# Seven products for eight: Strassen's algorithm in the first matrix of both MLPs, with two of four weight sums made by accumulating DMA transfers

## The chip, the cores and the metric

The kernel runs on one core of one Trainium2 chip. The metric is the device time of one execution in microseconds (us). PE is the matrix engine (TensorE) and PEld its weight load, ACT is ScalarE, DVE is VectorE, POOL is GpSimd, SP is the engine that issues most DMA transfers.

## The reference, cut to what matters

Two encoder layers over L = 16 + 512 tokens of width 1024. Each layer adds a mixer's output to the residual h, then an MLP's:

```python
u = rmsnorm(h, mlp_norm_g[layer])
h = h + jnp.square(jax.nn.relu(u @ w_ff1[layer])) @ w_ff2[layer]
return h[:, N_META:]
```

w_ff1 is 1024 x 4096 and w_ff2 is 4096 x 1024, in float32. The second layer's MLP works on the last 512 tokens only, since the others are dropped.

## The kernel before

Everything lies feature-major: a tile holds 128 features by all tokens. Every matrix product keeps nearly full float32 precision by splitting each operand into a rounded part and a remainder (xh and xl, wh and wl) and adding three products: wh·xh, wh·xl, wl·xh. A **unit** is one 128 x 1024 block of weights, 512 KB: SP loads `raw` (L207), ACT rounds it to `wh` (L208), DVE makes `wl` (L209), and `gemm` (L219) runs 8 k-steps x 3 products, in two halves of 264 tokens in the first layer (48 matmuls) or one piece of 512 tokens in the second (24).

The stages in order of time: the mixer of layer 0 (to 349 us), its output projection O0 (8 units), the MLP M0 (to 769 us), the mixer of layer 1, whose last part is the second half of its output projection (`c_out(4, KT)`, 8 half units), and the MLP M1 (974 us to the end).

An MLP runs in four quarters q of the hidden width. In each, 8 units of the first matrix W1 give 8 activation blocks (relu on ACT, times itself on DVE, then split into ah and al), and 8 units of the second matrix W2 use them; their results are added up in `facc` (L1133), and in the last quarter multiplied by `r2` (the squared norm factor, from `sum_squares` and a matmul with constants) and added to h. `make_x` (L1060, L1061) multiplies h by the norm's gain and splits it.

Tile pools give the memory: `wp` holds two buffers each of raw, wh and wl through the whole kernel. In PSUM, four tiles of two banks (`dn`) serve both MLPs. The text is written in a certain order, but a planner decides each engine's final order when the program is made: it takes the work that it expects to be ready, earlier text first, and an engine then runs its queue in order. A pool opened with `reuse_waits="tile"` over memory of a closed one waits tile by tile for what lay there.

Of the kernel before, what the change touches and what calls it, by code (L numbers as in the profile page):

```python
# [8 lines left out]
F32 = mybir.dt.float32  # L9
# [8 lines left out]
P = 128  # L18
# [116 lines left out]
def build(tc, ins, out, dbg=None):  # L135
# [14 lines left out]
    wp = ctx.enter_context(tc.tile_pool(name="wp", bufs=2, side="left"))  # L150
    xp = ctx.enter_context(tc.tile_pool(name="xp", bufs=1, side="left"))
    dp = ctx.enter_context(tc.tile_pool(name="dp", bufs=1, space=DRAM))

    psum = {}
# [46 lines left out]
    def load_unit(src):  # L201

        k, m = src.shape[1], src.shape[2]
        raw = wp.tile([P, k, m], F32, name="raw", tag="raw")
# [820 lines left out]
        tap(f"yA{h}", yA[h])  # L1025
    tap("yB", yB)
    ab_cm.__exit__(None, None, None)
    psum_pool("psm0", dn=4)
    if dbg is not None and "_ab" in dbg:
        for j in range(4):  # L1030
# [16 lines left out]
    hk = [h[:, k, :] for k in range(KT)]  # L1047
    yh, yl = [], []
    for k, s in enumerate(yA + [yB[:, j, :] for j in range(4)]):
        a, b = hl_tile(k, False), hl_tile(k, True)  # L1050
# [14 lines left out]
    def sum_squares(pool, t0=0):  # L1065

        sq = None
        for k in range(KT):
            s = pool.tile([P, L], F32, name="sqk", tag="sqk", bufs=2)
            S.activation(out=s[:, t0:], in_=hk[k][:, t0:], func=AF.Square)  # L1070
            if k:
                t = pool.tile([P, L], F32, name="sqa", tag="sqa", bufs=2)
# [5 lines left out]
    xs = []  # L1078
    for m in range(KT):
        hr = mp.tile([P, L], F32, name="hr", tag="hr", bufs=2)  # L1080
        nc.sync.dma_start(out=hr, in_=ins["h0"][:, m, :])
        ps = ps_dense()
        gemm(full(ps), load_unit(ins["w_o0"][m]), yh, yl)
        V.tensor_tensor(out=tokview(hk[m]), in0=ps[:, :, :HL], in1=tokview(hr), op=ALU.add)
        xs.append(make_x(m, PK_G + 8))
    yp_cm.__exit__(None, None, None)
    tap("h1", h)

    def mlp(layer, t0, xs, final):
        lp_cm = tc.tile_pool(name=f"mlp{layer}", bufs=1, side="right", reuse_waits="tile")  # L1090
        lp = lp_cm.__enter__()
        acc = lp.tile([P, KT, L], F32, name="facc")
        xh, xl = [x[0] for x in xs], [x[1] for x in xs]
# [10 lines left out]
        r2 = None  # L1104
        for q in range(4):
            ah, al = [], []
            for m in range(8):
                ps = ps_dense()
                gemm(dst(ps), load_unit(ins[f"w1_{layer}"][q * 8 + m]), xh, xl)
                rl = lp.tile([P, L], F32, name="rl", tag="rl", bufs=2)  # L1110
                S.activation(out=tview(rl), in_=pview(ps), func=AF.Relu)  # L1111
                V.tensor_tensor(out=tview(rl), in0=tview(rl), in1=pview(ps), op=ALU.mult)  # L1112
                a, b = hl_tile(m, False), hl_tile(m, True)
                S.copy(out=a[:, t0:], in_=rl[:, t0:])  # L1114
                V.tensor_tensor(out=b[:, t0:], in0=rl[:, t0:], in1=a[:, t0:], op=ALU.subtract)  # L1115
                ah.append(a)
                al.append(b)
            if q == 1:
                sq = sum_squares(lp, t0)
# [5 lines left out]
                V.reciprocal(out=r2[:, t0:], in_=r2[:, t0:])  # L1125
            for m in range(8):
                ps = ps_dense()
                gemm(dst(ps), load_unit(ins[f"w2_{layer}"][q * 8 + m]), ah, al)
                ak = acc[:, m, :]
                if q == 0:  # L1130
                    S.copy(out=tview(ak), in_=pview(ps))
                else:
                    V.tensor_tensor(out=tview(ak), in0=tview(ak), in1=pview(ps), op=ALU.add)  # L1133
                if q == 3:
                    V.tensor_tensor(out=ak[:, t0:], in0=ak[:, t0:], in1=r2[:, t0:], op=ALU.mult)
                    V.tensor_tensor(out=hk[m][:, t0:], in0=hk[m][:, t0:], in1=ak[:, t0:], op=ALU.add)
                    final(m)
        lp_cm.__exit__(None, None, None)

    mark("M0")  # L1140
    xs2 = []
    mlp(0, 0, xs, lambda m: xs2.append(make_x(m, PK_G + 16)))
    tap("h2", h)
    xh, xl = [x[0] for x in xs2], [x[1] for x in xs2]


    mark("L1")
    psum_pool("psc", dn=2, pw=2, po=1, cq=1)
    cp_cm = tc.tile_pool(name="cp", bufs=1, side="right", reuse_waits="tile")
    cp = cp_cm.__enter__()  # L1150
    rope = cp.tile([P, 2, L], F32, name="rope")
# [1 line left out]
    cst_ = {}  # L1153

    def stats():
        sq = sum_squares(cp)
# [141 lines left out]
        yl.append(b)  # L1298
        yield

    xs = []

    def c_out(k0, k1):

        for m in range(KT):
            mark("O1")
            ps = ps1("cq") if k0 == 0 else ps1(("cq", "po")[m % 2])
            gemm([(ps, slice(NM, L))], load_unit(ins["w_o1"][m][:, k0:k1, :]), yh[k0:k1], yl[k0:k1])
            V.tensor_tensor(out=hk[m][:, NM:], in0=ps, in1=hk[m][:, NM:], op=ALU.add)
            if k1 == KT:  # L1310
                xs.append(make_x(m, PK_G + 24, NM))
            yield


# [5 lines left out]
    next(streams["k0"])  # L1320
    stats()
    trace(streams, ORDER_C)
    weave((c_out(4, KT), 1))
    cp_cm.__exit__(None, None, None)
    tap("h3", h)

    psum_pool("psm1", dn=4)
    mark("M1")
    mlp(1, NM, xs, lambda m: nc.sync.dma_start(out=out[m], in_=hk[m][:, NM:]))
    psum_pool(None)  # L1330
    ctx.close()

# [74 lines left out]
```

## Time and profile before

| | us |
|---|---|
| median of 3 runs (1334.22, 1339.44, 1339.55) | 1339.44 |
| the profiled execution | 1335.85 |
| its span, first to last instruction | 1334.1 |
| PE busy in the span | 1299.1 (97%) |
| DVE busy | 754.9 (57%) |
| ACT busy | 558.6 (42%) |

Matmuls are pipelined, so the busy time of one is longer than the distance to the next. That distance, here called the pitch, is what a stream of matmuls costs for each.

### The profile page before, as it was taken

To read this page: it belongs to the slowest core of one execution; us is meant where nothing else is said; L and a number is where in the kernel's file an instruction comes from. 1 tells how busy PE (TensorE), PEld (TensorE's weight loads), DVE (VectorE), ACT (ScalarE), POOL (GpSimd) and SP (SyncE) were. 2 spreads that over 40 slices of the span, in tenths; PEclk is the share of its full clock that TensorE was granted. 3 is DMA by queue.
4 is the path that set the end of the run, shared out by engine and by line. 5 is a ranking of instruction groups with operands and counts; after the bars stand their busy time and mean duration, and the time that the engine had idled before them with its cause. 6 is when DMAs were issued, how large, how long until landed. Compare 5 with 4: busy or idle time off the path is not lost.

```text
span 1334.1 us, 21206 instructions
## 1 busy us (share of the span) xinstructions
PE 1299.1 (97%) x8595; PEld 1180.8 (89%) x8595; DVE 754.9 (57%) x1575; ACT 558.6 (42%) x1084; POOL 88.1 (7%) x202
## 2 busy tenths in 40 slices
PE   7998999899999999999999999999999999999998
PEld 6997999789899999999999987988788888888886
DVE  5686868986554324434335668698663244343444
ACT  4634565556533323223123357576443232231331
POOL 1051506030000000000000000000000000000000
PEclk9998999999899999999999999999999999999999
DMA  4321212100143323332332221101243333333333
GB/s 170 113 64 32 65 33 65 48 2 3 49 126 95 96 83 93 95 91 85 95 96 87 88 85 43 56 16 33 71 117 94 98 95 92 95 95 102 95 97 98
DMA packets 32081, 105.20 MB, mean 79 GB/s; under 512 B 3688, under 2 KB 3816, under 8 KB 31856
## 3 DMA queue, kind: packets, MB, share of 16 engines
q1 hardware_dynamic: 31984, 103.86, 25.9%
q8 instruction: 67, 1.10, 0.4%
q14 instruction: 30, 0.25, 0.1%
HBM read 101.73 MB, written 2.11 MB: 78 GB/s over the span
## 4 chain that ended last, share of the span: by engine, by line
PE 88%; DVE 5%; ACT 3%; POOL 2%; issue 1%; DMA 1%; SPq 0%; ACTq 0%; DVEq 0%
PE dn L219 64%; PE cq L219 5%; PE po L1292 2%; PE dn L1265 2%; PE pw L980 1%; PE pw L1286 1%; POOL u L634 1%; DVE cy L429 1%; POOL ut L633 1%; PE po L219 1%; PE rw L735 1%; PE rw L668 1%; PE rw L682 1%; PE pw L464 1%; PE rw L723 1%
## 5 line engine op out<-in xcount | busy, mean ns | idle before, releaser
L208 ACT CAST wh<-raw 128x1024 fp32r<-128x1024 f32 (+1 forms) x186 | 188.3, 1012 | 479.9 <-PE dn L219 416.7
L209 DVE TENSOR_TENSOR wl<-raw,wh 128x1024 fp32r<-128x1024 f32 (+1 forms) x186 | 219.9, 1182 | 254.0 <-ACT wh L208 249.5
L219 PE MATMUL dn<-xh,wh 128*128 128x264 f32 (+1 forms) x1184 | 297.4, 313 | 1.1 <-ACT wh L208 0.9
L219 PE MATMUL dn<-xh,wl 128*128 128x264 f32 (+1 forms) x1184 | 294.4, 312 | 0.0
L219 PE MATMUL dn<-xl,wh 128*128 128x264 f32 (+1 forms) x1184 | 294.3, 310 | 0.0
L219 PE MATMUL dn<-ah,wh 128*128 128x264 f32 (+1 forms) x896 | 232.3, 318 | 0.0
L219 PE MATMUL dn<-ah,wl 128*128 128x264 f32 (+1 forms) x896 | 230.6, 316 | 0.0
L219 PE MATMUL dn<-al,wh 128*128 128x264 f32 (+1 forms) x896 | 229.4, 314 | 0.0
L219 PEld LDWEIGHTS dn<-xl,wh 128*128 128x128 f32 x1184 | 195.7, 191 | 12.1
L219 PEld LDWEIGHTS dn<-xh,wh 128*128 128x128 f32 x1184 | 195.3, 191 | 12.4 <-issue 1.1
L219 PEld LDWEIGHTS dn<-xh,wl 128*128 128x128 f32 x1184 | 194.0, 190 | 11.1 <-issue 0.2
L219 PEld LDWEIGHTS dn<-al,wh 128*128 128x128 f32 x896 | 148.3, 189 | 11.9 <-issue 0.2
L219 PEld LDWEIGHTS dn<-ah,wh 128*128 128x128 f32 x896 | 148.0, 190 | 10.8 <-ACT ah L1051 0.3
L219 PEld LDWEIGHTS dn<-ah,wl 128*128 128x128 f32 x896 | 147.0, 188 | 11.0
L1133 DVE TENSOR_TENSOR facc<-facc,dn 128x528 f32<-128x528 f32 (+1 forms) x48 | 33.3, 693 | 129.8 <-PE dn L219 129.8
L1114 ACT CAST ah<-rl 128x528 fp32r<-128x528 f32 (+1 forms) x64 | 40.1, 627 | 89.3 <-DVE rl L1112 89.3
L1115 DVE TENSOR_TENSOR al<-rl,ah 128x528 fp32r<-128x528 f32 (+1 forms) x64 | 44.8, 701 | 43.2 <-ACT ah L1114 43.0
L1112 DVE TENSOR_TENSOR rl<-rl,dn 128x528 f32<-128x528 f32 (+1 forms) x64 | 44.1, 689 | 0.0
L429 DVE SCALAR_TENSOR_TENSOR cy<-cin,pk,cy 128x526 f32<-128x526 f32 (+1 forms) x48 | 38.2, 797 | 1.3 <-ACT cy L426 1.0
L1111 ACT ACTIVATE rl<-dn 128x528 f32<-128x528 f32 (+1 forms) x64 | 38.2, 597 | 0.0
L633 POOL TENSOR_TENSOR ut<-abc,u 128x150 f32<-128x150 f32 (+14 forms) x60 | 29.8, 497 | 93.8 <-DVE abc L625 89.5
L1224 POOL MEMSET cvt<- 128x128 f32 x2 | 0.4, 204 | 526.2 <-PE pw L457 526.2
(447 smaller groups left out, 1726.9 us busy)
## 6 DMA issues: line engine op xcount, KB each, us to landing
raw<-in_w SPq DMA_DIRECT2D x128, 512.0 KB, 3.6
raw<-in_w_in SPq DMA_DIRECT2D x22, 512.0 KB, 3.7
raw<-in_w_c SPq DMA_DIRECT2D x12, 512.0 KB, 3.6
raw<-in_w_o SPq DMA_DIRECT2D x8, 512.0 KB, 3.7
raw<-in_w_o SPq DMA_DIRECT2D x16, 256.0 KB, 2.7
gcb<-gdram SPq DMA_DIRECT2D x8, 264.0 KB, 4.5
hr<-in_h SPq DMA_DIRECT2D x8, 264.0 KB, 2.7
out<-h SPq DMA_DIRECT2D x8, 256.0 KB, 2.0
```

The lines of the kernel that those rows point to most:

```text
L208: S.copy(out=wh, in_=raw)
L209: V.tensor_tensor(out=wl, in0=raw, in1=wh, op=ALU.subtract)
L219: T.matmul(o, a[:, k, :], b[k][:, sl], start=first and k == 0 and i == 0, stop=last and k == n - 1 and i == 2)
L429: V.scalar_tensor_tensor(out=y[:, a:a + n], in0=x[:, b:b + n], scalar=w(j), in1=y[:, a:a + n], op0=ALU.mult, op1=ALU.add)
L633: G.tensor_tensor(out=ut[:, :, :, :n], in0=arow, in1=ucol, op=ALU.mult)
L1111: S.activation(out=tview(rl), in_=pview(ps), func=AF.Relu)
L1112: V.tensor_tensor(out=tview(rl), in0=tview(rl), in1=pview(ps), op=ALU.mult)
L1114: S.copy(out=a[:, t0:], in_=rl[:, t0:])
L1115: V.tensor_tensor(out=b[:, t0:], in0=rl[:, t0:], in1=a[:, t0:], op=ALU.subtract)
L1133: V.tensor_tensor(out=tview(ak), in0=tview(ak), in1=pview(ps), op=ALU.add)
L1265: T.matmul(ps[:, s, :HL], a[:, sl], b[:, s * HL:(s + 1) * HL], start=i == 0, stop=i == 2)
L1292: T.matmul(po, a[:, kc, :], b, start=kc == 0 and i == 0, stop=kc == NC and i == 2)
```

## The change

For each pair of W1 units, seen as 2 x 2 blocks (two column blocks of weights, two halves of the 1024 inputs) against 2 x 2 blocks of the input (two halves of the inputs, two halves n of the tokens: n = 264 in the first layer, 256 in the second), Strassen's algorithm in Winograd's form takes 7 products of half size for 8. Each product still has three matmuls for each of 4 k-steps.

The sums of inputs (T1 to T4) are made once, by `Fast.add`, in O0 and in `c_out`. The sums of weights are made for each pair: two by accumulating DMA transfers that GpSimd issues onto blocks which SP loaded, two on DVE. The results come together from PSUM: ACT copies partial sums out (e0 to e3), and PE goes on accumulating on the same bank. h is parked in DRAM during the MLP and read back by GpSimd's queue, and the W2 sums use h's own memory in the place of `facc`. Weight pools are now opened and closed stage by stage; the MLP's has 5 buffers for wh and wl.

```diff
+    def weight_pool(name, bufs=2):
+        if "cm" in wpool:
+            wpool.pop("cm").__exit__(None, None, None)
+        if name is not None:
+            wpool["cm"] = tc.tile_pool(name=name, bufs=bufs, side="left", reuse_waits="tile")
+            wpool["p"] = wpool["cm"].__enter__()
+        return wpool["p"]
...
+        def add(self, k):
...
+            if k < 4:
+                x = self.temp.tile([P, L], F32, name=f"xf{k}")
+                S.activation(out=x[:, t0:], in_=hk[k][:, t0:], func=AF.Copy, scale=g)
+                self.split("B11", i, a[:, t0:m], b[:, t0:m], x[:, t0:m])
+                self.first[i] = x
+                V.tensor_tensor(out=x[:, t0:m], in0=x[:, t0:m], in1=x[:, m:], op=ALU.subtract)
+                self.split("T1", i, a[:, m:], b[:, m:], x[:, t0:m])
+                return
+            x, hs = self.first.pop(i), hk[k]
+            S.activation(out=a[:, t0:], in_=hs[:, t0:], func=AF.Copy, scale=g)
+            V.scalar_tensor_tensor(out=b[:, t0:], in0=hs[:, t0:], scalar=g, in1=a[:, t0:], op0=ALU.mult, op1=ALU.subtract)
...
+            V.scalar_tensor_tensor(out=t2, in0=hs[:, m:], scalar=g, in1=x[:, t0:m], op0=ALU.mult, op1=ALU.add)
+            self.split("T2", i, *part("T2"), t2, -1.0)
+            V.scalar_tensor_tensor(out=t3, in0=hs[:, m:], scalar=g, in1=x[:, m:], op0=ALU.mult, op1=ALU.subtract)
+            self.split("T3", i, *part("T3"), t3)
+            V.scalar_tensor_tensor(out=t4, in0=hs[:, t0:m], scalar=g, in1=t2, op0=ALU.mult, op1=ALU.subtract)
+            self.split("T4", i, *part("T4"), t4, -1.0)
...
+            def load(name, i):
+                raw = wp.tile([P, 3, 4, P], F32, name="raw", tag="raw", bufs=2)
+                w = ins[f"{name}_{layer}"]
+                nc.sync.dma_start(out=flat(raw[:, 0:2]), in_=w[i])
+                if name == "w2":
+                    return raw, None
+                s = wp.tile([P, 4, 4, P], F32, name="sums", tag="sums", bufs=2)
+                nc.sync.dma_start(out=s[:, 1], in_=w[i][:, :4])
+                nc.sync.dma_start(out=s[:, 2], in_=w[i + 1][:, 4:])
+                nc.sync.dma_start(out=raw[:, 2], in_=w[i + 1][:, 4:])
+                for k in (1, 2):
+                    G.dma_start(out=s[:, k], in_=w[i + 1][:, :4], accum_op=ALU.add)
+                return raw, s
...
+                yield split(flat(raw[:, 0:2]))
+                if w == "w2":
+                    continue
+                V.tensor_tensor(out=s[:, 3], in0=s[:, 2], in1=raw[:, 0], op=ALU.add)
+                yield split(flat(s[:, 2:4]))
+                V.tensor_tensor(out=s[:, 0], in0=s[:, 3], in1=raw[:, 1], op=ALU.add)
+                yield split(flat(s[:, 0:2]))
+                yield split(raw[:, 2])
...
+        def product(o, g, half, name, start):
+            wh, wl = groups[g]
+            for k in range(4):
+                xh, xl = fast.ops[name][k]
+                for i, (a, b) in enumerate(((wh, xh), (wh, xl), (wl, xh))):
+                    T.matmul(o, a[:, half * 4 + k, :], b, start=start and k == 0 and i == 0, stop=k == 3 and i == 2, skip_group_check=not start)
+        def activated(m, c):
+            S.activation(out=c[:, t0:], in_=c[:, t0:], func=AF.Square)
+            a, b = hl_tile(m, False), hl_tile(m, True)
+            S.copy(out=a[:, t0:], in_=c[:, t0:])
+            V.tensor_tensor(out=b[:, t0:], in0=c[:, t0:], in1=a[:, t0:], op=ALU.subtract)
+            return a, b
+        def pair(base, m, before):
...
+            prepare()
+            product(pa, base, 0, "B11", True)
+            S.copy(out=e[0], in_=pa)
+            product(pb, base, 1, "B21", True)
+            used.add(base)
+            V.tensor_tensor(out=c0[:, lo], in0=e[0], in1=pb, op=ALU.add)
+            before()
+            prepare()
+            product(pa, base + 1, 1, "T2", False)
+            S.copy(out=e[1], in_=pa)
+            product(pd, base + 1, 0, "T1", True)
+            used.add(base + 1)
+            S.copy(out=e[2], in_=pd)
+            prepare()
+            product(pa, base + 2, 1, "T3", False)
+            S.copy(out=e[3], in_=pa)
+            V.tensor_tensor(out=c1[:, hi], in0=e[3], in1=e[2], op=ALU.add)
+            product(pd, base + 2, 0, "B22", False)
+            used.add(base + 2)
+            S.activation(out=c1[:, hi], in_=c1[:, hi], func=AF.Relu, scale=-1.0)
+            V.tensor_tensor(out=c0[:, hi], in0=e[1], in1=pd, op=ALU.add)
+            S.activation(out=c0[:, t0:], in_=c0[:, t0:], func=AF.Relu)
+            acts[m] = activated(m, c0)
+            def end():
+                prepare()
+                product(pa, base + 3, 0, "T4", False)
+                used.add(base + 3)
+                S.activation(out=c1[:, lo], in_=pa, func=AF.Relu, scale=-1.0)
+                acts[m + 1] = activated(m + 1, c1)
+            return end
...
+                if q == 3:
+                    o = lp.tile([P, L], F32, name="last", tag="c0", bufs=2)
+                    V.tensor_tensor(out=tview(o), in0=tview(r2), in1=pview(ps), op=ALU.mult)
+                    V.tensor_tensor(out=ak[:, t0:], in0=ak[:, t0:], in1=o[:, t0:], op=ALU.add)
                     final(m)
```

`prepare` takes the next groups of split weights while fewer than 5 are open; `pair` is called with the former pair's `end` as `before`, so that the product T4 of a pair stands among the next pair's.

## Rows read from the trace of the kernel before

**Rows 1.** Busy time of each engine in M0 and in M1, clock, DMA.

```profile
core 0: us, PE busy (x) PEld busy (x) DVE busy (x) ACT busy (x) POOL busy (x), PEclk, DMA share, GB/s
398.00:769.00 371.00, 371.00 (x3076) 370.87 (x3075) 156.75 (x177) 113.94 (x145) 0.00 (x0) 1.00 0.31 91
974.20:1329.20 355.00, 354.76 (x1538) 288.30 (x1537) 149.16 (x172) 106.82 (x137) 0.00 (x0) 1.00 0.32 97
```

**Rows 2.** Chain of work that ended last, in order of time: start, duration, count.

```profile
537.80 231.26 PE dn L219 x1918
...
974.19 133.12 PE dn L219 x576
...
1108.17 220.80 PE dn L219 x960
```

**Rows 3.** The same chain in the mixer of layer 1: transposes of 128 columns.

```profile
939.42 0.87 PE pw L1286 x8
940.29 2.96 PE cq L219 x12
```

**Rows 4.** ACT, groups by shape: count, busy us, mean ns, idle time before.

```profile
L208 ACT CAST wh<-raw 128x1024 fp32r<-128x1024 f32 x170 | 178.3, 1049 | 461.3 <-PE dn L219 416.7 <-issue 38.5 <-PE cq L219 3.2
...
L1114 ACT CAST ah<-rl 128x528 fp32r<-128x528 f32 x32 | 20.3, 634 | 44.7 <-DVE rl L1112 44.7
...
L1111 ACT ACTIVATE rl<-dn 128x528 f32<-128x528 f32 x32 | 19.3, 604 | 0.0
...
L208 ACT CAST wh<-raw 128x512 fp32r<-128x512 f32 x16 | 9.9, 621 | 18.6 <-PE cq L219 15.6 <-ACT sqk L1070 3.0
L1070 ACT ACTIVATE sqk<-h 128x528 f32<-128x528 f32 x16 | 9.8, 633 | 0.8 <-DVE sqa L1073 0.8
...
L319 ACT COPY gt<-rw 32x264 f32<-32x264 f32 x2 | 0.7, 368 | 6.3 <-PE rw L318 6.3
```

**Rows 5.** DVE, groups by shape.

```profile
L209 DVE TENSOR_TENSOR wl<-raw,wh 128x1024 fp32r<-128x1024 f32 x170 | 208.9, 1229 | 254.0 <-ACT wh L208 249.5 <-PE dn L1122 2.5
...
L1115 DVE TENSOR_TENSOR al<-rl,ah 128x528 fp32r<-128x528 f32 x32 | 22.7, 708 | 21.8 <-ACT ah L1114 21.7
...
L1061 DVE SCALAR_TENSOR_TENSOR xl<-h,pk,xh 128x528 fp32r<-128x528 f32 x16 | 12.2, 765 | 6.4 <-ACT xh L1060 6.4
L209 DVE TENSOR_TENSOR wl<-raw,wh 128x512 fp32r<-128x512 f32 x16 | 10.9, 683 | 0.0
...
L592 DVE TENSOR_TENSOR dt<-pw,dt 128x256 f32<-128x256 f32 x16 | 6.1, 413 | 0.0
...
L1084 DVE TENSOR_TENSOR h<-dn,hr 128x528 f32<-128x528 f32 x8 | 5.7, 708 | 20.6 <-PE dn L219 20.6
```

**Rows 6.** ACT's timeline, four casts in a row.

```profile
348.08 2.22 ACT L1051 CAST ah<-yA 128x528 fp32r<-128x528 f32 x4
```

**Rows 7.** DVE's timeline, four subtractions in a row.

```profile
349.26 2.56 DVE L1052 TENSOR_TENSOR al<-yA,ah 128x528 fp32r<-128x528 f32 x4
```

**Rows 8.** ACT's timeline where O0 passes into M0.

```profile
398.83 0.73 ACT L1060 ACTIVATE xh<-h,pk 128x528 fp32r<-128x528 f32 x1
399.47 0.63 ACT L1070 ACTIVATE sqk<-h 128x528 f32<-128x528 f32 x1
403.66 1.05 ACT L208 CAST wh<-raw 128x1024 fp32r<-128x1024 f32 x1 [3.57 <-issue]
404.62 0.60 ACT L1111 ACTIVATE rl<-dn 128x528 f32<-128x528 f32 x1
```

**Rows 9.** DMA issues by line: KB each, median us from issue to landing.

```profile
raw<-in_w SPq DMA_DIRECT2D x128, 512.0 KB, 3.6
...
raw<-in_w_o SPq DMA_DIRECT2D x16, 256.0 KB, 2.7
gcb<-gdram SPq DMA_DIRECT2D x8, 264.0 KB, 4.5
```

**Rows 10.** SP's timeline in O0: a W1 unit's load.

```profile
382.85 0.33 SPq L207 DMA_DIRECT2D raw<-in_w  x1
```

**Rows 11.** Busy time and clock where the first mixer ends.

```profile
340.00:352.00 12.00, 9.68 (x58) 7.98 (x57) 6.47 (x24) 8.79 (x28) 0.00 (x0) 0.81 0.00 1
```

More of the change, by code (lines that the diff above doesn't have):

```diff
@@ L1047, in build @@
     hk = [h[:, k, :] for k in range(KT)]
+    hdram = [dp.tile([P, KT, L], F32, name=f"hdram{i}") for i in range(2)]
     yh, yl = [], []
@@ L1063, in make_x, with __init__, split @@
         return a, b
-    def sum_squares(pool, t0=0):
+    class Fast:
+        def __init__(self, pool, temp, gcol, t0):
+            self.pool, self.temp, self.gcol, self.t0, self.n = pool, temp, gcol, t0, (L - t0) // 2
+            self.first, self.ops = {}, {n: [None] * 4 for n in ("B11", "B21", "B22", "T1", "T2", "T3", "T4")}
+        def split(self, name, i, a, b, src, sign=1.0):
+            S.activation(out=a, in_=src, func=AF.Copy, scale=sign)
+            if sign == 1.0:
+                V.tensor_tensor(out=b, in0=src, in1=a, op=ALU.subtract)
+            else:
+                V.scalar_tensor_tensor(out=b, in0=src, scalar=sign, in1=a, op0=ALU.mult, op1=ALU.subtract)
+            self.ops[name][i] = (a, b)
+        def add(self, k):
+            t0, n, g = self.t0, self.n, pkc(self.gcol + k)
+            m, i = t0 + n, k % 4
+            a = xp.tile([P, L], F32R, name=f"xh{k}", tag=f"xh{k}")
+            b = xp.tile([P, L], F32R, name=f"xl{k}", tag=f"xl{k}")
+            fresh = lambda name: self.temp.tile([P, HL], F32, name=name, tag=name, bufs=2)[:, :n]
+            part = lambda name: [self.pool.tile([P, HL], F32R, name=f"{name}{c}{i}")[:, :n] for c in "hl"]
+            if k < 4:
[9 more added lines that the diff above has]
+            V.scalar_tensor_tensor(out=b[:, t0:], in0=hs[:, t0:], scalar=g, in1=a[:, t0:], op0=ALU.mult, op1=ALU.subtract)
+            self.ops["B21"][i] = (a[:, t0:m], b[:, t0:m])
+            self.ops["B22"][i] = (a[:, m:], b[:, m:])
+            t2, t3, t4 = fresh("t2"), fresh("t3"), fresh("t4")
+            V.scalar_tensor_tensor(out=t2, in0=hs[:, m:], scalar=g, in1=x[:, t0:m], op0=ALU.mult, op1=ALU.add)
[4 more added lines that the diff above has]
+            self.split("T4", i, *part("T4"), t4, -1.0)
@@ L1076, in sum_squares, with park @@
         return sq
-    xs = []
+    def park(layer, k, t0=0):
+        G.dma_start(out=hdram[layer][:, k, t0:], in_=hk[k][:, t0:])
+    fq_cm = tc.tile_pool(name="fq0", bufs=1, side="left", reuse_waits="tile")
+    fq = fq_cm.__enter__()
+    ft_cm = tc.tile_pool(name="ft0", bufs=1, side="left", reuse_waits="tile")
+    fast = Fast(fq, ft_cm.__enter__(), PK_G + 8, 0)
+    weight_pool("wo0")
     for m in range(KT):
@@ L1102, in tview, with reload @@
             return tokview(ap) if t0 == 0 else ap[:, t0:]
-        r2 = None
-        for q in range(4):
[L1106 to L1117, printed above, removed]
+        def reload(m):
+            o = mp.tile([P, L], F32, name="hr", tag="hr", bufs=2)[:, t0:]
+            G.dma_start(out=o, in_=hdram[layer][:, m, t0:])
+            return o
@@ new lines, in weight_groups, with split @@
+        def weight_groups():
+            def split(src):
+                k = src.shape[1]
+                wh = wp.tile([P, KT, P], F32R, name="wh", tag="wh", bufs=RING)
+                wl = wp.tile([P, KT, P], F32R, name="wl", tag="wl", bufs=RING)
+                S.copy(out=wh[:, :k], in_=src)
+                V.tensor_tensor(out=wl[:, :k], in0=src, in1=wh[:, :k], op=ALU.subtract)
+                return wh, wl
+            def load(name, i):
[11 more added lines that the diff above has]
+                return raw, s
+            flat = lambda t: t.rearrange("p a k m -> p (a k) m")
+            todo = []
+            for q in range(4):
+                todo += [("w1", q * 8 + m) for m in range(0, 8, 2)] + [("w2", q * 8 + m) for m in range(8)]
+            loaded = [load(*todo[0])]
+            for i, (w, m) in enumerate(todo):
+                if i + 1 < len(todo):
+                    loaded.append(load(*todo[i + 1]))
+                raw, s = loaded.pop(0)
+                yield split(flat(raw[:, 0:2]))
[6 more added lines that the diff above has]
+                yield split(raw[:, 2])
@@ new lines, in mlp, with prepare @@
+        source = weight_groups()
+        groups, used = [], set()
+        def prepare():
+            while len(groups) < RING or len(groups) - RING in used:
+                g = next(source, None)
+                if g is None:
+                    return
+                groups.append(g)
+        def product(o, g, half, name, start):
[4 more added lines that the diff above has]
+                    T.matmul(o, a[:, half * 4 + k, :], b, start=start and k == 0 and i == 0, stop=k == 3 and i == 2, skip_group_check=not start)
@@ L1118, in mlp @@
+        r2, base = None, 0
+        for q in range(4):
+            acts = {}
+            end = lambda: None
+            for m in range(0, 8, 2):
+                end = pair(base, m, end)
+                base += 4
+            end()
             if q == 1:
-                sq = sum_squares(lp, t0)
+                sq = sum_squares(lp, reload, ("c0", "c1"))
                 ps = ps_dense()
@@ L1155, in stats @@
     def stats():
-        sq = sum_squares(cp)
+        sq = sum_squares(cp, lambda k: hk[k])
         ps = ps_dense()
@@ L1310, in c_out @@
             if k1 == KT:
-                xs.append(make_x(m, PK_G + 24, NM))
+                park(1, m, NM)
+                fast.add(m)
             yield
```

66 lines of the change are left out of this document (49 added, 17 removed).

## The prediction

> **What bounds the kernel now.** I first read the busy time by stage. In both MLPs PE is busy for practically the whole stretch (371.00 of 371.00 us, 354.76 of 355.00), at the full granted clock, while ACT and DVE are busy for less than half of it [rows 1]. The chain of waits says the same: through both MLPs it runs along L219 almost without a break [rows 2]. So an MLP lasts as long as its matmuls take, and a matmul that is left out is worth one pitch, as long as the other engines keep up and nothing new stops PE.
>
> The pitch comes from the chain: 231.26 us for 1918 matmuls of 264 columns is 120.6 ns; (133.12 + 220.80) us for 576 + 960 of 512 columns is 230.4 ns [rows 2]. A line through both has 0.443 ns a column, and gives 117.0 ns at 256 columns, a width that no MLP row has.
>
> Last I read the order on ACT's queue, since the change hangs on it. A cast of weights (403.66) runs ahead of the relu (404.62) that stands before it in the text, and a square of `sum_squares`, written after the second quarter, runs at 399.47 in O0 [rows 8]. So the planner doesn't keep the written order; it fills an engine with what is ready.
>
> **What is removed.** A pair of W1 units had 96 matmuls in M0 and has 84 (7 products x 4 k-steps x 3). There are 16 pairs: 16 x 12 x 0.1206 = 23.1 us. In M1 a pair had 48 matmuls of 512 columns, 11.06 us, and gets 84 of 256: 84 x 0.1170 = 9.83 us, so 16 x 1.23 = 19.7 us. Bounds for M1: if the cost went by columns alone (0.1152), 22.1 us; if 256 columns cost as much as 264, 14.9 us. Would the weight load set the pitch, since M1 now loads weights 84 times and not 48? Eight transposes, each with fresh weights, go by in 0.87 us, 109 ns apart [rows 3], below 117. Together 42.8 us.
>
> The Trainium skill (TensorE: Matmul & The Clock Gate, section Back-to-back issue gap) puts an isolated gap at N/2.4 + 2.5 ns, which would be 112.5 ns at 264 columns and 109.2 at 256. By it the saving would be 40.6 us as an estimate. The measured pitch [rows 2] is 7% longer at 512 and 264 alike, and I take the rows.
>
> The last unit's tail gets shorter: one DVE pass in place of a sum (0.708, [rows 5]) at the end of either MLP, 1.4 us.
>
> **What ACT and DVE must do in a pair's time.** By durations [rows 4, 5], for a pair in M0. ACT: three casts of 1024 columns (3.147), one of 512 (0.621), six operations on 264 columns (e0 to e3 and two relus, 2.208 by the row of 264), a relu (0.604), two squares and two casts of 528 (2.534): 9.11 us. DVE: three remainders of 1024 (3.687), one of 512 (0.683), two weight sums (1.366), three sums of 264 (1.239 by the row of 256), two remainders of 528 (1.416): 8.39 us. PE needs 84 x 0.1206 = 10.13. Operations in a row overlap: four casts took 2.22 us, 0.53 apart for 0.63 each [rows 6], and four subtractions 2.56, 0.62 apart for 0.70 [rows 7]. With 0.10 off each of 15 operations and 0.08 off each of 11, ACT needs 7.6 us and DVE 7.5. Both fit, at three quarters of PE's time, where they are under half now. If their work is hidden it costs nothing; but PE now waits for them inside a pair: T3 goes onto the bank that e1 is copied from, and only T1 (12 x 0.1206 = 1.45 us) lies between. A copy takes 0.37 us, an unlucky cast of 1.05 ahead of it makes 1.42, and with the handing over PE stops for a few tenths, unless it has the next pair's B11 to do. Bounds: nothing, and 1.0 us a pair. I take 0.2, since the order is by readiness: 32 x 0.2 = 6.4 us.
>
> **The transfers in the steady state.** A pair now loads 1.25 MB by SP and 0.5 MB by GpSimd, where it loaded 1 MB. The DMA engines' share of 0.31 [rows 1] becomes 0.31 x 1.75 x 11.58 / 10.13 = 0.62. An accumulating transfer of 256 KB is in no row: between a plain one, 2.7 us, and the slowest of that size, 4.5 [rows 9]. SP's loads can start when the buffers of two pairs ago are free; with groups split five ahead, that is two pairs and three products, 2 x 10.13 + 4.3 = 24.6 us, before T2 reads the first sum. Casting and summing take 3.0 of it. Loads and both accumulations one after another take at most 3.6 + 3 x 2.7 + 2 x 4.5 = 20.7. So they are hidden. Behind an accumulation on GpSimd's queue stand only the parked h and the next accumulation. The loads of h for the squares and for the third quarter's sum go past with slack of several units.
>
> **Where PE stops: the two entries.** Now W1's first weights are loaded during O0 (382.85, [rows 10]) from a pool that stays. After the change the MLP's pool is opened over `Fast.add`'s temporaries and the closed projection pool, and waits for them tile by tile. In the order of allocation, the memory for sums lies over the temporaries t3 and t4 and over O0's raw weights. After the last matmul of O0 (398.0) these take h 0.708, xh 0.73, xl 0.765, then T2 to T4 with six more operations of 0.41 and one of 0.37 on the way, some 4.6 us [rows 5, 8]. Then a load (2.7), the accumulations (2.7 to 4.5), and sum, cast and remainder (0.683 + 1.049 + 1.229 = 2.96): T2 can start 13.0 to 14.8 us after O0. PE has the two products B11 and B21 of the first pair and of the next to do, 5.8 us; it stops for 7 to 9. Bounds: 0 if the memory doesn't collide, 12 if the next pair isn't taken ahead. I take 8.
>
> At M1 the sums' memory lies over the projection's last weights, free when PE is done with them: 2.7 + 2.7 to 4.5 + 2.96 = 8.4 to 10.2 us, less 4 x 12 x 0.117 = 5.6 of products. Besides, `add` costs DVE in the last four half units of `c_out` about 4.6 us each (0.683 for the weights, 0.683, 0.765, six of 0.41), against 12 x 0.2304 = 2.77 on PE: DVE comes 4.5 (back to back) to 7.4 us late into M1. I take 6, from 3 to 12. O0 itself opens a new pool too: load, cast and remainder, 3.6 + 1.05 + 1.23 = 5.9 us at most; its memory is that of tiles used some us before the first mixer's end, so I take 0.
>
> Where PE had been idle, 9.68 busy of 12.00 us, the granted clock was 0.81 [rows 11], a mixture of the levels 2.4 and 1.2 GHz. The stops at the entries should show this too. I add 2 us, from 0 to 4. The Trainium skill says the same of idleness (TensorE: Matmul & The Clock Gate, Part 1: The HAM clock gate); it adds no term.
>
> **The sum**, against the profiled execution: 1335.85 - 42.8 - 1.4 + 6.4 + 8 + 6 + 2 = 1314.0. The median lies 3.6 us above that execution (1339.44), so 1317.6, rounded to 1318 us.
>
> **Rivals.**
>
> *ACT and DVE set the pair's time (slower or the same).* In the written order each engine would wait for the other, from one T4 to the next: relu 0.368, square 0.633, cast 0.634, cast 1.049, remainder 1.229, sum 0.683, cast 1.049, remainder 1.229, sum 0.683, cast 1.049, remainder 1.229, two sums 0.826, relu 0.604, square 0.633, cast 0.634, cast 0.621, copy 0.368: 13.52 us, against 11.58 and 11.06 now. With 12 of 16 pairs so (the last of a quarter prepares W2's weights, the first has no former T4), 12 x (1.94 + 2.46) = 52.8 lost, the other pairs' gain of 4 x (1.45 + 1.23) = 10.7 kept: 1335.85 + 52.8 - 10.7 - 1.4 + 16 + 3.6 = 1396. Rows 8 speak against it in full. In part it can be: the planner goes by expected durations, and engines keep its order when the real ones differ. It decides from (42.8 + 1.4 - 16) / 32 = 0.88 us lost a pair; at 1.3 us the time is 1353. Chance 0.20.
>
> *The entries are hidden (faster still).* If the first loads find free memory, no more than 3 us is left of the entries and clock: 1335.85 - 42.8 - 1.4 + 6.4 + 3 + 3.6 = 1305, with 1299 where no pair loses anything. Against it: a pool of three times the former size can't lie clear of what was just closed. Chance 0.12.
>
> *The sums come late.* If each accumulation took 10 us, 3.6 + 8.1 + 20 + 3 = 34.7 us would not fit in 24.6, and with 10 us over, spread on the two pairs that the buffers span, a pair would lose 5: 24 pairs behind another pair x 5 = 120 us, about 1440. It begins at 5 us each. For it: no row has an accumulation. Against it: the slowest plain row is 4.5. Chance 0.05.
>
> **How the numbers follow.** My forecast has 0.63: 1300 to 1335 (bounds: M1's pitch -2.4 to +4.8, entries 3 to 24, pairs 0 to 16 us). A measurement of this kernel can tell about 0.5%, 6.7 us. Faster, below 1332.7: 0.58 of the forecast's 0.63 and the hidden entries, 0.70. Same: the forecast's rest and a third of the first rival, 0.12. Slower, above 1346.1: 0.18. The range for 8 in 10 leaves out the low end of the hidden entries and the worse part of the rivals: 1298 to 1352.
>
> **What the profile after would show.** W1 stretches with matmuls of 264 columns 0.12 us apart and of 256 at 0.117, PE idle under 0.3 us a pair; ACT and DVE about three quarters busy there; two breaks of 6 to 9 us on PE at 398 and at about 960, with a wait for a load or an accumulation and a clock below 1; accumulations landing in 3 to 5 us. Wrong would be: PE waiting in every pair for ACT's copies or for split weights, a pitch at 256 that stays at 0.12, or no breaks at the entries.

## The result, and the profile after

The changed kernel takes 1458.69 us (median of 4 runs, 1456.48 to 1462.12), the one before 1336.83 in the same session: 1.091 times, 95% interval [1.088, 1.095]. The prediction was 1318, range 1298 to 1352. It was wrong in sign and by 141 us. The profiled execution took 1456.48 us (span 1454.6).

PE's W1 quarters come first: busy time in windows of the kernel after, filtered to the products' line, four of M0 and four of M1.

```profile
core 0: us, PE busy (x) PEld busy (x), PEclk, DMA share, GB/s
409.80:471.00 61.20, 48.59 (x336) 46.23 (x336) 0.85 0.74 181
518.60:566.50 47.90, 43.25 (x336) 41.64 (x336) 1.00 0.57 143
636.50:685.50 49.00, 44.41 (x336) 43.07 (x336) 0.97 0.54 135
733.60:784.30 50.70, 44.34 (x336) 43.09 (x336) 0.97 0.35 91
1040.40:1098.10 57.70, 48.88 (x336) 46.23 (x336) 0.83 0.71 181
1144.00:1193.50 49.50, 43.56 (x336) 41.76 (x335) 0.97 0.55 139
1259.30:1308.60 49.30, 43.55 (x336) 41.82 (x335) 0.97 0.53 138
1354.90:1405.50 50.60, 44.45 (x336) 43.19 (x335) 0.93 0.34 90
```

The matmuls that the change promises to leave out are gone: 336 a quarter, where there were 384 in M0 and 192 wider ones in M1. But at the rates of [rows 2] a quarter took 384 x 0.1206 = 46.3 and 192 x 0.2304 = 44.2 us; the six steady ones now take 48 to 51, with two stops of PE in each that make 4.6 to 6.3 us together, and the first ones 61.2 and 57.7. Before, PE had no such gaps [rows 1]. The eight quarters lose 208.8 - 185.2 = 23.6 us in M0 and 207.1 - 177.0 = 30.1 in M1, where the forecast had a gain of 42.8 less 6.4.

**Who stops PE in a steady quarter.** VectorE's groups by shape: count, busy us, mean ns, and the idle time just before them by what ended it. The first sum of each pair, and the second, which never waits:

```profile
L1232 DVE TENSOR_TENSOR sums<-sums,raw 128x512 f32<-128x512 f32 x32 | 22.1, 690 | 110.2 <-DMA sums<-in_w 58.5 <-DMA raw<-in_w 51.5
L1234 DVE TENSOR_TENSOR sums<-sums,raw 128x512 f32<-128x512 f32 x32 | 22.0, 688 | 0.5
```

VectorE stands 110 us before 32 small sums, 3.4 us each in the mean, until a transfer lands. This idle time is not yet a cost; it becomes one where other work stands behind the sum. The next rows follow one pair from its issue to PE's stop (timelines of SP, GpSimd, VectorE, ScalarE and PE, the last bracket is the idle time before the instruction):

```profile
529.00 0.33 SPq L1213 DMA_DIRECT2D sums<-in_w  x1
529.38 0.42 SPq L1214 DMA_DIRECT2D sums<-in_w  x1
...
532.12 1.77 POOL L1217 DMA_DIRECT2D sums<-in_w  x2 [17.73 <-DMA sums<-in_w]
...
534.89 1.22 DVE L1202 TENSOR_TENSOR wl<-raw,wh 128x1024 fp32r<-128x1024 f32 x1 [0.54 <-ACT wh L1201]
539.62 0.69 DVE L1232 TENSOR_TENSOR sums<-sums,raw 128x512 f32<-128x512 f32 x1 [3.50 <-DMA sums<-in_w]
...
543.72 0.42 DVE L1288 TENSOR_TENSOR c<-e,e 128x264 f32<-128x264 f32 x1
...
544.18 0.42 ACT L1291 ACTIVATE c<-c 128x264 f32<-128x264 f32 x1 [2.98 <-DVE c L1288]
...
545.74 0.36 ACT L1274 COPY e<-dn 128x264 f32<-128x264 f32 x1
...
546.16 0.39 PE L1254 MATMUL dn<-xh,wh 128*128 128x264 f32 x1 [3.07 <-ACT e L1274]
...
549.04 1.04 ACT L1201 CAST wh<-sums 128x1024 fp32r<-128x1024 f32 x1
...
558.93 0.34 PE L1254 MATMUL dn<-T2h,wh 128*128 128x264 f32 x1
```

Two accumulations are issued at 532.12 and land by 539.6. The planner has put the sum ahead of an addition of the running pair, L1288, and VectorE keeps that order: it stands 3.50 us at the sum, does sums and remainders, and comes to L1288 at 543.72. ScalarE's Relu waits 2.98 us for that, PE 3.07 us for the copy behind the Relu. Yet this sum belongs to the next pair, the last of the quarter: its result is cast at 549.04 and read by PE's T2 at 558.93, 19 us after the landing. The sum came in time for PE; it stood too early in VectorE's queue. In that quarter (518.6 to 566.4) VectorE is busy for 26.3 us and ScalarE for 30.2 of 47.8.

DMA issues of the kernel after: count, KB each, median us to landing (compare [rows 9]).

```profile
raw<-in_w SPq DMA_DIRECT2D x96, 512.0 KB, 4.1
sums<-in_w SPq DMA_DIRECT2D x64, 256.0 KB, 2.8
sums<-in_w POOLq DMA_DIRECT2D x64, 256.0 KB, 5.7
```

An accumulating transfer takes 5.7 us (4.0 to 8.4 over the 64), twice a plain one of that size. I had 2.7 to 4.5.

**The late squares.** Timelines of GpSimd (loads of h), ScalarE (squares) and PE where the second quarter ends, and the windows of two stretches there (all engines, then clock and DMA):

```profile
573.64 0.57 POOL L1191 DMA_DIRECT2D hr<-hdram  x1 [9.73 <-ACT sqk L1143]
575.65 0.55 POOL L1191 DMA_DIRECT2D hr<-hdram  x1 [1.44 <-ACT sqk L1143]
...
577.26 0.64 ACT L1143 ACTIVATE sqk<-hr 128x528 f32<-128x528 f32 x1 [1.91 <-DMA hr<-hdram]
...
586.52 2.13 PE L1317 MATMUL dn<-sqa,onesd 128*128 128x264 f32 x4 [19.84 <-DVE sqa L1146]
```

```profile
566.50:588.00 21.50, 1.66 (x6) 1.18 (x4) 10.21 (x13) 10.24 (x17) 3.85 (x7) 0.63 0.53 162
571.90:592.40 20.50, 5.88 (x22) 5.47 (x23) 10.27 (x11) 5.31 (x8) 3.85 (x7) 0.50 0.44 137
```

The squares ran in O0 before [rows 8]; now h comes back through two buffers, and load, square and addition go by turns of some 2 us, seven of them in this stretch, after the pairs have given c0 and c1 free. The squares' matmul (L1317) stands ahead of W2's in PE's queue: PE stands 19.8 us in M0 and 18.1 in M1. From 571.90 to 592.40 the granted clock is 0.50, 1.2 GHz, where PE had stood since 566.7, and W2's first matmuls still run at it. The Trainium skill (TensorE: Matmul & The Clock Gate, Part 1: The HAM clock gate) says that idleness lowers the clock; this trace agrees, with 0.50 in that stretch.

**The entry of M0**, by PE's stops and ScalarE's casts ahead of them:

```profile
408.72 1.03 ACT L1201 CAST wh<-raw 128x1024 fp32r<-128x1024 f32 x1
...
409.80 0.59 PE L1254 MATMUL dn<-xh,wh 128*128 128x264 f32 x1 [4.89 <-ACT wh L1201]
...
422.30 2.00 ACT L1201 CAST wh<-sums 128x1024 fp32r<-128x1024 f32 x2 [8.26 <-DVE sums L1232]
...
423.40 0.59 PE L1254 MATMUL dn<-xh,wh 128*128 128x264 f32 x1 [7.24 <-ACT wh L1201]
```

It has two long stops, 4.89 and 7.24 us; M1 has three, 3.25 in the last projection and 3.29 and 3.09 in its first quarter. A further stop in each first quarter (3.87 and 3.56 us) waits for the copy L1274, as in the steady quarters, and is gone when the accumulations are left out. Ahead of O0 there is a stop of 4.9 that I had put at 0, with these rows of ScalarE and PE:

```profile
349.30 2.22 ACT L1067 CAST ah<-yA 128x528 fp32r<-128x528 f32 x4
351.43 2.23 ACT L1067 CAST ah<-yB 128x528 fp32r<-128x528 f32 x4
353.56 1.99 ACT L221 CAST wh<-raw 128x1024 fp32r<-128x1024 f32 x2
...
354.66 0.81 PE L232 MATMUL dn<-ah,wh 128*128 128x264 f32 x2 [4.88 <-ACT wh L221]
```

The first weights' cast stands behind the eight casts of the mixer's results, though their load had landed at 346.3, before PE stopped at 349.8.

### The profile page after: what moved, and what is told of

Its sections match the earlier page's. It is cut to its first block, busy times and chain, and to the rows that moved or that the text cites. A ratio compares the mean times of both kernels' runs of the same rounds, so it can differ in the third digit from the quotient of the medians.

```text
span 1454.6 us, 23004 instructions
## 1 busy us (share of the span) xinstructions
PE 1307.6 (90%) x8979; PEld 1201.0 (83%) x8979; DVE 882.3 (61%) x1815; ACT 703.9 (48%) x1412; POOL 170.7 (12%) x314
## 5 line engine op out<-in xcount | busy, mean ns | idle before, releaser
L1254 PE MATMUL dn<-xh,wh 128*128 128x264 f32 (+1 forms) x512 | 156.9, 307 | 45.3 <-ACT e L1274 26.6
L1202 DVE TENSOR_TENSOR wl<-raw,wh 128x1024 fp32r<-128x1024 f32 (+1 forms) x128 | 139.3, 1089 | 59.5 <-ACT wh L1201 57.2
L1254 PE MATMUL dn<-xh,wl 128*128 128x264 f32 (+1 forms) x512 | 150.7, 297 | 2.0 <-DVE wl L1202 2.0
L1254 PE MATMUL dn<-xl,wh 128*128 128x264 f32 (+1 forms) x512 | 151.3, 296 | 0.0
L1254 PEld LDWEIGHTS dn<-xh,wh 128*128 128x128 f32 x512 | 103.6, 202 | 53.6 <-ACT e L1274 32.6
L1254 PEld LDWEIGHTS dn<-xh,wl 128*128 128x128 f32 x512 | 102.9, 202 | 3.2 <-DVE wl L1202 3.2
L1254 PEld LDWEIGHTS dn<-xl,wh 128*128 128x128 f32 x512 | 103.4, 202 | 0.1
L232 PE MATMUL dn<-xh,wh 128*128 128x264 f32 x416 | 91.7, 297 | 1.0 <-DVE last L1339 0.8
L232 PE MATMUL dn<-xl,wh 128*128 128x264 f32 x416 | 90.4, 293 | 0.0
L232 PE MATMUL dn<-xh,wl 128*128 128x264 f32 x416 | 89.4, 293 | 0.0
L1232 DVE TENSOR_TENSOR sums<-sums,raw 128x512 f32<-128x512 f32 x32 | 22.1, 690 | 110.2 <-DMA sums<-in_w 58.5
```

The source lines that it names most:

```text
L232: T.matmul(o, a[:, k, :], b[k][:, sl], start=first and k == 0 and i == 0, stop=last and k == n - 1 and i == 2)
L1202: V.tensor_tensor(out=wl[:, :k], in0=src, in1=wh[:, :k], op=ALU.subtract)
L1232: V.tensor_tensor(out=s[:, 3], in0=s[:, 2], in1=raw[:, 0], op=ALU.add)
L1254: T.matmul(o, a[:, half * 4 + k, :], b, start=start and k == 0 and i == 0, stop=k == 3 and i == 2, skip_group_check=not start)
```

## The experiments

Each ratio is to the kernel before in the same session (its median 1335.5 to 1336.3), with its 95% interval.

**Is it the transfers? Leave them out, or make the sums by an engine.** `x1_no_acc` leaves the two accumulations out (its sums lack a term):

```
-                for k in (1, 2):
-                    G.dma_start(out=s[:, k], in_=w[i + 1][:, :4], accum_op=ALU.add)
```

> The two accumulating transfers of each pair are left out; the blocks they would add to are used as loaded, so the weight sums are incomplete. Two theories. Queue: DVE runs its queue in order, the planner puts the weight sums early on it, and DVE stops at them until a late transfer has landed (58.5 us in 12 waits for accumulations, 51.5 us in 11 for plain loads, in the changed kernel); PE then waits for the sums and copies queued behind. Load: ACT and DVE simply have too much to do in a pair's time, however the sums are made. Queue expects the later W1 quarters, now 47.7 to 50.6 us, to fall to 43 to 45, the two first ones (61.0 and 57.7) by about 10, and the whole to 1395 to 1415 us. Load expects under 10 us of change, 1450 or more.

1385.67 us, 1.037 [1.035, 1.040]: 73 us less. The steady quarters of M0 fall to 42.9 to 43.1 us, and no stop over 1 us is left in them. It is lower than I expected, and the load theory is out. VectorE still stands 50.4 us before the same sums, 47.8 of them for plain loads (51.5 before): those waits stop nothing, and the cost lies with the accumulations' waits.

`x3_pool_sums` and `x4_dve_sums` load both units whole and make the two sums on GpSimd, or on VectorE (which then makes all four):

```
+                nc.sync.dma_start(out=flat(raw[:, 5:7]), in_=w[i + 1])
+                E.tensor_tensor(out=raw[:, 2], in0=raw[:, 6], in1=raw[:, 5], op=ALU.add)
+                E.tensor_tensor(out=raw[:, 5], in0=raw[:, 0], in1=raw[:, 5], op=ALU.add)
```

> GpSimd adds the two sums in SBUF from plain loads, in the place of the accumulating transfers; each pair loads 1 MB and not 1.75. Queue theory: the sums are there earlier (a load of 3.6 to 4.1 us and two additions of some 1.5 us, estimated from 0.5 us for 150 columns, against a load and 4 to 8.4 us of accumulation), so DVE stops less: 1390 to 1415. Load theory: ACT and DVE do the same work as before, 1450 or more.

1426.75 us, 1.070 [1.067, 1.073]. A miss: GpSimd's sums come late too, with VectorE's waiting 25.5 us for them, and 20 of VectorE's 64 sums took 1.4 to 1.8 us in place of 0.69 (last section).

> DVE makes all four sums, from plain loads. Queue theory: DVE has 2 x 0.68 us more to do in a pair, but waits only for loads: 1400 to 1430. Load theory: 32 pairs x 1.37 us more, near 1500.

1387.08 us, 1.039 [1.037, 1.040], under its range and as fast as with the accumulations left out, though VectorE has 64 more operations. Windows on the products' line, M0:

```profile
413.00:462.00 49.00, 47.52 (x336) 45.52 (x336) 0.89 0.31 103
508.30:551.30 43.00, 42.87 (x336) 41.38 (x336) 1.00 0.25 80
619.60:662.30 42.70, 42.68 (x336) 41.46 (x336) 1.00 0.24 75
709.00:751.50 42.50, 42.50 (x336) 41.38 (x336) 1.00 0.26 79
```

PE stands no more in the steady quarters, which are under the 46.3 of before, as in `x1_no_acc`. More work on VectorE, at no cost: its load was never the bound.

**Is it the place in the queue, or a lead that is too short?** `x9_late_sums` keeps all transfers and asks for the first sum only behind the last addition of the pair before:

```
+                with tc.issue_after(late[0]) if late else nullcontext():
                     V.tensor_tensor(out=s[:, 3], in0=s[:, 2], in1=raw[:, 0], op=ALU.add)
...
-            prepare()
             product(pa, base + 1, 1, "T2", False)
...
-            prepare()
             product(pa, base + 2, 1, "T3", False)
```

> The changed kernel with its accumulating transfers and all its bytes, but VectorE's sums of a pair are asked for only near the end of the pair before, behind that pair's last addition, so that VectorE no longer stands at them while work of the pair waits behind. Theory (order of the queue): the stops inside the pairs go or shrink to half, 1390 to 1420 us. Rival (the transfers themselves come too late whatever the order): VectorE stands as long at the same sums, and the time stays at 1440 us or more.

1442.67 us, 1.081 [1.079, 1.083]. VectorE's idle time at that sum:

```profile
L1233 DVE TENSOR_TENSOR sums<-sums,raw 128x512 f32<-128x512 f32 x32 | 22.0, 686 | 34.4 <-DMA raw<-in_w 17.3 <-DMA sums<-in_w 17.1
```

110.2 becomes 34.4, yet only 16 us are won: the idle time shrank as in the theory, the time is the rival's. Asked for so late, the sums' splits come late instead, and PE stops for those (0.4 to 0.8 us at a time in M0's third quarter). The edit does two things, since it also takes two of a pair's `prepare` out and so asks for all splits later; which of them cost the rest is not told apart. Holding the sum back in this way is not the remedy. So the lead: `x12_sums_ahead` has three sum buffers filled a pair sooner, paid for with a ring of four split weights; `x13_ring4` is its control.

```
-    RING = 5
+    RING = 4
...
-                s = wp.tile([P, 4, 4, P], F32, name="sums", tag="sums", bufs=2)
+                s = wp.tile([P, 4, 4, P], F32, name="sums", tag="sums", bufs=3)
...
+            sums = [load_sums(pairs.pop(0)), load_sums(pairs.pop(0))]
```

> The changed kernel with its accumulating transfers, but the buffers of the sums are three instead of two and filled one pair sooner; the room comes from a ring of four instead of five split weights. Theory (the lead is too short): the stops inside the pairs go, and the time falls by 40 us or more against the same kernel with a ring of four and two buffers, to 1395 to 1420 us. Rival (GpSimd's queue or the memory can't carry the transfers however early they start): the fall is under 15 us, 1440 us or more.

> The changed kernel with a ring of four split weights in place of five and nothing else, the control of the one before. All theories: a shorter ring gives weights less lead, 1455 to 1485 us.

1425.79 us, 1.068 [1.066, 1.071], against 1463.22, 1.098 [1.092, 1.104]: 37 us for one pair of lead, a little less than I asked for. A second and a third quarter of M0, of the first kernel and then of its control:

```profile
513.60:557.40 43.80, 43.13 (x336) 41.47 (x336) 1.00 0.63 154
626.90:672.70 45.80, 43.15 (x336) 41.52 (x336) 1.00 0.61 148
```

```profile
521.30:573.10 51.80, 44.68 (x336) 43.02 (x336) 0.97 0.54 130
643.10:692.90 49.80, 44.61 (x336) 42.99 (x336) 0.97 0.57 136
```

With lead, a quarter of 43.8 us stands beside a DMA share of 0.63: neither the memory nor GpSimd's queue forbids these transfers. Nor are they faster there: an accumulation takes 6.2 us in the median. They came too late for the place of the first sum in VectorE's queue.

**The squares.** `x2_sq_early` takes them, with their matmul, at each MLP's start from h in its buffer:

```
-                sq = sum_squares(lp, reload, ("c0", "c1"))
+        sq = sum_squares(lp, lambda k: hk[k][:, t0:], ("c0", "c1"))
```

> The sum of squares, its matmul and r2 are made at the start of each MLP from h in SBUF, not after the second quarter from h read back from DRAM. If the reload through two buffers on GpSimd's queue is what PE waited for (gaps of 19.8 and 18.1 us, at a clock that then falls), 38 to 45 us go away: 1413 to 1421. Rival: the eight squares and seven sums only move to the entries, where ACT and DVE are late already, and half comes back: about 1438.

1427.76 us, 1.070 [1.066, 1.074], between the two theories. The late stops are gone, but the squares' matmul now stands in PE's queue at the entry: 4.2 us in M0 and 21.7 in M1. `x6_dve_sq`, on `x4_dve_sums`, spreads the squares over the first quarter, adds them in place and leaves the matmul where it was:

```
+                if q == 0:
+                    square(m)
+                    square(m + 1)
```

> All four weight sums on VectorE, and the squares of h taken in the first quarter, two after each pair, from h in its buffer (nothing read back for them) and summed in place. Late squares cost what the trace shows: stops of 19.0 and 17.4 us at the end of the second quarters of the kernel with all sums on VectorE (1387 us), each followed by a stretch at the low clock. Theory: both go, nothing takes their place: 1340 to 1352 us. Rival: VectorE and ScalarE have no room for 16 more operations in the first quarter, and the first quarters grow by what the second ones lose: 1370 us or more.

1350.81 us, 1.012 [1.010, 1.014]: 36.3 less than `x4_dve_sums`, all that the theory asked for. It takes away both the late place of the squares and the way through DRAM; the two aren't told apart.

**The entries.** `x7_dve_entry` is `x4_dve_sums` with the rings first in the pool and raw weights behind them, in free memory; `x8_dve_sq_entry` has this and the spread squares.

```
+        first = [[wp.tile([P, KT, P], F32R, name=w, tag=w, bufs=RING) for w in ("wh", "wl")]]
```

> All four weight sums on VectorE, and in each MLP's weight pool the rings of the parts come first and the buffers of the raw weights behind them, in memory that nobody holds, so the first loads don't wait for the products' temporaries. Theory: the stops of 9.2 us before the first MLP and of 3.4 and 4.5 us before the second are those loads, and most of them goes: 1370 to 1378 us. Rival: the stops are VectorE's work on the last parts of h, and the time stays within 3 us of 1387 us.

> Both changes of the two kernels before it together: all sums on VectorE, squares in the first quarter, raw weights in free memory. If the three costs are separate, they add: 1324 to 1340 us, at or below the time of the kernel before. Rival: the squares and the entry use the same slack of VectorE, and the gain of the second is lost: 1345 us or more.

1382.88 us, 1.035 [1.034, 1.037], and 1348.09, 1.009 [1.008, 1.011]. Both miss. The first load leaves 15 us sooner, but the stop at M0 only shrinks from 9.2 to 4.9 us: the cast stands behind the last part of h. With the squares it was 7.3: they are ready and went first. `x10_held_sq` holds the squares back behind a pair's work; `x11_early_group` also splits the first weights ahead of the last part and moves the temporaries away from O0's weights:

```
+                    with tc.issue_after(late[0]), tc.issue_after(late[1]):
                         square(m)
                         square(m + 1)
```

```
+        groups, used = [next(source)], set()
+        fast.add(KT - 1)
```

> All sums on VectorE, raw weights in free memory, squares in the first quarter but each two held behind the last addition and the Relu of a pair, so that they can't go ahead of the first weights' cast. In the kernel without the hold (1348 us) the squares stood among the last parts of h: first stop 7.3 us against 4.9 us with late squares, and slower second weights. Theory: the stop falls back to 4.9 us and the time to 1342 to 1346 us. Rival: the held operations push the first pairs' own work, and the time is 1347 us or more.

> The kernel before with two more moves: the temporaries of the products' parts lie on the other side of memory, so that the output projection's weights are loaded sooner, and the first weights of each MLP are split before the parts of the last tile of h are made. Theory: the stop before the output projection (4.9 us) and those at the two entries (4.9 and 3.3 to 3.5 us) mostly go, each with its time at the low clock: 1328 to 1338 us, level with the kernel before. Rival: they are not set by these loads and casts, 1341 us or more.

1349.95 us, 1.011 [1.009, 1.013], and 1354.75, 1.014 [1.012, 1.017]: no gain, and a loss. The stop at M0 did go to 4.9 and to 3.1, but what was moved came back behind it, in the first quarters and their W2. These reorderings do not help. That there is too much to do at once is so far only argued.

So take the work away from there. `x14_last_three` multiplies the first quarter by eight products, with the x of the kernel before, makes T2 to T4 beside it and T1 at its end. It left out the subtraction that T2 and T4 need; `x15_last_three_b` has it.

```
+            for m in range(8 if q == 0 else 0):
+                prepare()
+                ps = ps_dense()
+                gemm(dst(ps), groups[base], [x[0] for x in xs], [x[1] for x in xs])
...
+                if m % 2:
+                    fast.parts(m // 2)
```

> Seven products in the last three quarters of each MLP only. The first quarter goes by eight, as in the kernel before, and the parts of h are made beside it; the sums of weights on VectorE, the squares in the first quarter. Theory (what keeps the repaired kernel at 1348 us is the work at the entries): the entries are those of the kernel before again, and each of six quarters gives what the repaired kernel's later quarters gave, 3.7 us (46.2 to 42.5) and 2.7 us (44.0 to 41.3): 1336 - 11.1 - 8.1 = 1317, at 1313 to 1326 us. Rival (the seven products' own cost in the quarters, or VectorE's load): no gain, 1333 us or more.

> The kernel with seven products in the last three quarters again, with the subtraction that T2 and T4 need (four more operations of VectorE in each MLP's first quarter; the one before left them out). The entries theory gives the time that it had, 1325 to 1333 us, under the kernel before; if those operations were on the path it would be 1334 us or more.

1329.29 us, 0.996 [0.995, 0.998], and 1330.28, 0.996 [0.994, 0.997]: 5.3 us faster than the kernel before (1335.56), and 18 faster than `x8_dve_sq_entry`. It is the only form of the change found here that gains, by a little less than the 0.5% I had set as the bound. The first three W1 quarters of M0 of `x15_last_three_b` (all engines):

```profile
405.70:452.00 46.30, 46.30 (x387) 46.30 (x386) 30.05 (x54) 32.33 (x59) 0.79 (x2) 1.00 0.29 86
498.20:541.20 43.00, 42.85 (x339) 41.51 (x338) 29.62 (x41) 29.90 (x54) 0.00 (x0) 1.00 0.24 74
589.90:633.00 43.10, 43.03 (x339) 41.65 (x338) 30.46 (x41) 30.26 (x54) 0.00 (x0) 1.00 0.23 75
```

M0's first quarter is that of before again, with no stop. The expected 1317 isn't reached: three stops remain that the kernel before has not, 4.9 us before O0, 3.6 at M1's entry and 1.3 in W2. They make 9.8 of the 13 us that are missing. `x16_first_proj` loads and splits O0's first weights ahead of the mixer's results:

```
+    weight_pool("wo0")
+    wo_first = [load_unit(ins["w_o0"][0])]
```

> The same, and the output projection's first weights are loaded and split ahead of the eight splits of the mixer's results, behind which their cast stood while TensorE stopped for 4.9 us. Theory: 3 to 5 us less than without, 1321 to 1329 us. Rival: the load lands too late for any other place, the time stays.

1329.99 us, 0.996 [0.994, 0.997]; that stop went from 4.87 to 4.34 only. The load does not set it. In `x11_early_group` the load is issued at 324.99 us and lands at 329.22, 21 us before PE stops, and the stop is 4.87 as ever. It is the cast's place in ScalarE's queue, behind the eight casts of the mixer's results; `x16_first_proj` brought it ahead of only one of them. In the kernel before, O0's first weights are loaded at 221.4 and cast at 229.7, long before those eight. A run with the cast ahead of all eight was not made.

## Why the prediction was wrong

The loss of 123.2 us (1458.7 against 1335.5) by the runs, each of which keeps the repairs of the row before; the runs are of several sessions:

| step | from, to | us |
|---|---|---|
| accumulating transfers | 1458.7 to 1387.1 (`x4_dve_sums`) | 71.6 |
| squares late and read back | to 1350.8 (`x6_dve_sq`) | 36.3 |
| memory of the first loads | to 1348.1 (`x8_dve_sq_entry`) | 2.7 (the two intervals overlap) |
| left over against the kernel before | to 1335.5 | 12.6 |

**The step that failed** is "So they are hidden", on the transfers: it had the wrong reader. It compared a chain of 20.7 us with a lead of 24.6 up to T2, and for T2 that came out. In the 30 pairs behind the first of either MLP the chain, from SP's first load of a pair's sums to the landing of the second accumulation, took 9.3 to 14.8 us, and both accumulations had landed 11 to 89 us before the pair's first T2 matmul. An accumulation takes 5.7 us and not 4.5 at most, but that isn't what failed: `x12_sums_ahead` is 37 us faster than its control with accumulations of 6.2. What reads the transfer first is VectorE's sum, early in VectorE's queue, before work of the running pair. A queue that is kept in order turns a late transfer into a stop of everything behind it, long before its result is due on PE. In sum the accumulations cost 71.6 us, 2.2 a pair; one more pair of lead gives about half of it back.

I had a part of that in hand: "engines keep its order when the real ones differ" stands in the first rival. The third rival, with 0.05, had the right transfers and the wrong condition: it makes them late for T2, and "It begins at 5 us each" by that measure. Outside the two first pairs, which it counts as entries, they never were.

**The loads of h** "go past with slack of several units": they don't, 36.3 us. I had looked at GpSimd's queue and not at the two buffers, nor at c0 and c1, which the squares share with the pairs. I had read that a square ran in O0 [rows 8], and put its move to the end of the second quarter at nothing, without a reason.

**Readiness.** "The order is by readiness", I wrote, and it was no comfort: the planner goes by the times that it expects, the engines keep its order, and what was ready (squares in `x8_dve_sq_entry`) went ahead of what was urgent.

**Small waits in a pair.** 0.2 us was too little. In `x4_dve_sums` a steady quarter of M0 takes 42.5 to 43.0 us for 336 x 0.1206 = 40.5: 0.5 to 0.6 a pair, in many waits of a tenth or two on a bank that is being copied. So a quarter gives 3.7 us at best, and in M1, where `x15_last_three_b` takes some 41.3 of 44.2, 2.9; eight quarters give 26, not 36. The mechanism was right in kind, a wait for ScalarE's copies, but T3 on e1's bank is the smaller part of it: in M0's second quarter of `x4_dve_sums` PE's starts are late by 2.0 us in all, 0.6 of it at T3's first matmuls and 1.2 at the first matmuls behind the copy of e0.

**The entries.** Right in place, too small, and right in cause only in part. M0's two stops make 4.89 + 7.24 = 12.1 us for 8 (bounds 0 to 12), M1's three 9.6 for 6 (3 to 12). The second of M0 waits for the first sum, as forecast. The first, before B11, does not hang on the load: with the load 15 us sooner it is still 4.9 (`x7_dve_entry`), since the cast stands behind the last part of h. (The operations listed for that part add up to 5.0 us one after another, not 4.6.) O0's stop is 4.9 for 0: I had reckoned with the load's time and not with the cast's place behind the mixer's casts. The clock shows the stops, with 0.85 and 0.83 in the first quarters; what it cost, for my 2 us, no run takes by itself. That the entries cost the last of the gain is shown by the pair `x8_dve_sq_entry` and `x15_last_three_b`: 18 us, of which 10 lie between O0's start and M0's end (422.5 us against 412.2) and 7 between the MLPs (213.2 against 206.2), where the parts of h were made for M1.

**What held.** The count of matmuls; 256 columns at 118 to 119 ns from start to start (median in the trace) where 117.0 was predicted; no limit by the weight load; and VectorE's and ScalarE's load, which is not the bound (`x4_dve_sums`): the rival with 0.20 was right that an engine's order can stop PE, and wrong on why. The Trainium skill's isolated gap (TensorE: Matmul & The Clock Gate, Back-to-back issue gap) would be 109.2 ns at 256 columns; the trace is 8% above it.

## What to carry to other kernels

A transfer is hidden only if it has landed when its first reader reaches the head of an in-order queue; compare its time with the place that the planner gave the reader, and ask who stands behind it. A fast algorithm adds work where the loop begins, when nothing can cover it: use it from the second block on and make its operands under the first. Adding on an engine with idle time (64 operations of 0.69 us) was cheaper than the transfer that was to save it.

## What I hadn't expected of the hardware

An accumulating transfer into SBUF of 256 KB took 5.7 us in the median (4.0 to 8.4), a plain one of that size 2.8 in the same kernel, and its issue kept GpSimd busy for about 0.9 us each (1.77 for two at 532.12). Why it takes twice as long stays open.

With sums on GpSimd (`x3_pool_sums`), VectorE's 64 additions of 128x512 fall into two groups: 44 take 0.68 to 0.69 us and 20 take 1.44 to 1.79. The 20 are exactly those that start while an addition on GpSimd is running, and each of them ends 0.55 us behind it. One that starts ahead of GpSimd's is not slowed, as the first of these three rows shows:

```profile
485.51 0.69 DVE L1229 TENSOR_TENSOR raw<-raw 128x512 f32<-128x512 f32 x1 [1.18 <-POOL raw L1213]
485.56 1.79 POOL L1214 TENSOR_TENSOR raw<-raw 128x512 f32<-128x512 f32 x1
...
486.24 1.66 DVE L1231 TENSOR_TENSOR raw<-raw 128x512 f32<-128x512 f32 x1
```
